# Tracing three score units of an attention beside the products of its values, in a two-layer diffusion trunk on one core

## The chip, the cores and the metric

The kernel runs on one core of a Trainium2 chip. The metric is the device time of one execution in microseconds (us). TensorE (PE in the rows) multiplies matrices, VectorE is DVE, ScalarE ACT, GpSimd POOL, and SyncE (SP) issues most transfers. Each engine works through an instruction queue of its own, fixed when the program is built, and instructions wait on semaphores that other engines raise.

## The reference

Two layers over 512 latent tokens and 256 context tokens, each with 1024 features. A layer normalises and modulates its input, projects it into four head groups, mixes each in its own way, projects the four results back and adds them; a convolutional channel mixer (ffn) follows.

```python
def attend(q, k, v, scale, sink=None):
    s = jnp.einsum('bqkgd,bnkd->bkgqn', q, k).astype(jnp.float32) * scale
    if sink is None:
        p = jax.nn.softmax(s, axis=-1)
    else:
        p = softmax_sink(s, sink)
    return jnp.einsum('bkgqn,bnkd->bqkgd', p.astype(v.dtype), v)
...
    ql = apply_axial_rope(rmsnorm(ql, q_norm), cos, sin)     # mixer A
    kl = apply_axial_rope(rmsnorm(kl, k_norm), cos, sin)
    kc = rmsnorm(kc, k_norm)
    k_all = jnp.concatenate([kl, kc], axis=1)
    v_all = jnp.concatenate([vl, vc], axis=1)
    y = dense_latent_attention(ql, k_all, v_all, scale)
```

Group A is a dense attention of four query heads over two key/value heads of 64 features. Group C is a banded one (keys within 128 positions, and the context) with a sink logit, B a state-space scan, D a latent attention. In layer 0 the context tokens are queries too.

## The kernel before

Everything stays in fp32 accuracy: an operand is split into a rounded high part and the rest (`hhi`/`hlo`, `whi`/`wlo`), and three products make one. `split` and `psplit` cast the high part on ACT and subtract on DVE (`split`) or POOL (`psplit`).

Per layer, `mixers` first makes the queries `aq0`, `aq1` and keys `ak` of A (the products `psf`, then sums `psn` and broadcasts `psr` for their norms, and DVE multiplications into `aq`, `ak`). Then come the values of A and C, six groups of 128 tokens with 24 products `psv` each; ACT copies each group into `vta` and `vtc`, DVE eight columns into `dtr`. Then `gqa` runs attention A in units of 128 queries, numbered u0, u1, ... in this text (in layer 0, 20 units: per head four latent ones of 768 keys and one of 2 x 128 context queries). A unit's scores are 4 products `pss`; DVE finds the negated maximum `nm`, ACT takes the exponential `p` and its sum, DVE inverts the sum, POOL multiplies (the function `scores`). LOOK = 3 units later `turn` transposes `p` through PE (`pspt`) and splits it, and `values` multiplies it with V (`psy`). Before its first scores a head pair needs `kh`/`kl` (the split keys) and `qh` (ACT casts the high half, POOL writes the low half by a subtraction); `get_kv` and `get_q` make them, and `prep` calls them for up to AHEAD = 10 units ahead.

Scores are in two PSUM tiles (`b2`), so u2 can begin when the exponential of u0 has read its tile. `psv`, `pspt`, `psy`, `psi` and `psn` share four smaller tiles (`b1`).

`run` takes streams with weights and interleaves what they trace: a stream of weight 0.3 advances 0.3 steps for each of one of weight 1. The build then simulates the traced program and fixes each engine's queue; an instruction behind a waiting one on the same engine waits too. Beside attention A runs `c_items`, the projections for C (`psi`); beside attention C run those of D and B.

Of the kernel before, what the change touches and what calls it, by code (L numbers as in the profile page):

```python
# [1 line left out]

# [1 line left out]

# [29 lines left out]
LOOK = 3  # L34
AHEAD = 10
NA, NC, NS = 0, 0, 12
WY = 4
WA, WC, WM, WD = 0.3, 0.3, 1.0, 1.0
# [4 lines left out]
STEP = 256  # L43
NP1 = 8
WP = 0.3
WQ, DQ = 0, 0
V0, V1, HC = 3, 0, 12
TK = 2
POOLK = (1, 3, 5, 7)
# [39 lines left out]
def trunk(ctx: ExitStack, tc: tile.TileContext, a, out):  # L89
# [22 lines left out]
    def s3(name, dt=F32, shape=(TOK,)):  # L112
        n = int(np.prod(shape))
        t = PW.tile([128, TOK], dt, tag="s3", name=name, bufs=N_S3)[:, :n]
        if len(shape) == 2:
            t = t.rearrange("p (a b) -> p a b", b=shape[1])
        elif len(shape) == 3:
            t = t.rearrange("p (a b c) -> p a b c", b=shape[1], c=shape[2])
        return t
# [20 lines left out]
    def psplit(hi, lo, src):  # L140
        act.copy(hi, src)
        pool.tensor_tensor(lo, src, hi.bitcast(F32), op=ALU.subtract)

    def run(*streams):

        live = [[g, w, 0.0] for g, w in streams]
        while live:
            s = min(live, key=lambda e: e[2])
            try:
                next(s[0])  # L150
                s[2] += 1.0 / s[1]
            except StopIteration:
                live.remove(s)
# [30 lines left out]
    def par_at(l, n, i=0, w=1):  # L184
        o, _ = POFF[n]
        return par[l][:, o + i:o + i + w]
# [253 lines left out]
    def gemm(items):  # L440

        posts = []

        def step():
            for g in list(posts):
                if next(g, posts) is posts:
                    posts.remove(g)

        w = items[0][0]()
        for i, (_, begin, *late) in enumerate(items):
            late = late[0] if late else 0
            quanta, post = begin(w)
            for q, _ in enumerate(quanta):
                if q == late and i + 1 < len(items):
                    w = items[i + 1][0]()
                step()
                yield
            if next(post, posts) is not posts:  # L460
                posts.append(post)
        while posts:
            step()
            yield
# [17 lines left out]
    def mixers(l, norm, halfway, mods):  # L482
# [124 lines left out]
        def once(f):  # L607
            box = []

            def g():  # L610
                if not box:
                    box.append(f())
                return box[0]

            return g

        def gqa(q, k, vt, sinkp, banded, ys):

            kmap = [(0, 256, 0), (512, 256, 256), (256, 256, 512)] if banded else [(0, TOK, 0)]
            cpos = 256 if banded else 512  # L620
            pos = (0, 1, 4, 5)
            halves = []
            for kv in range(2):
                r0 = slice(64 * kv, 64 * kv + 64)

                def get_kv(r0=r0, kv=kv):
                    kh, kl = s3("kh", F32R), s3("kl", F32R)
                    for s0, n, d0 in kmap:
                        for r in (slice(0, 64), slice(64, 128)):
                            act.copy(kh[r, d0:d0 + n], k[r0, s0:s0 + n])  # L630
                        for r in (slice(0, 64), slice(64, 128)):
                            pool.tensor_tensor(kl[r, d0:d0 + n], k[r0, s0:s0 + n], kh[r0, d0:d0 + n].bitcast(F32),
                                              op=ALU.subtract)
                    vhl = s3("vhl", F32R, (6, 128))
                    psplit(vhl[:, :, 0:64], vhl[:, :, 64:128], vt[:, :, 64 * kv:64 * kv + 64])
                    ys.append(s3("yf"))
                    return kh, kl, vhl, ys[-1]

                get_kv = once(get_kv)
                for hh in range(2):  # L640
                    hd = 2 * kv + hh
                    rh = slice(64 * hh, 64 * hh + 64)
                    rl = slice(64 - 64 * hh, 128 - 64 * hh)

                    def get_q(kv=kv, rh=rh, rl=rl):
                        qh = s3("qh", F32R)
                        act.copy(qh[rh, :QW], q[kv][rh, :QW])
                        pool.tensor_tensor(qh[rl, :QW], q[kv][rh, :QW], qh[rh, :QW].bitcast(F32), op=ALU.subtract)
                        return qh

                    get_q = once(get_q)

                    def prep(get_kv=get_kv, get_q=get_q):
                        get_kv()
                        get_q()

                    def sink(hd=hd):
                        return None if sinkp is None else (sinkp[0][:, hd:hd + 1], sinkp[1][:, hd:hd + 1])

                    def sc_mm(ps, q0, c0, w, masks=(), get_kv=get_kv, get_q=get_q):  # L660
                        kh, kl = get_kv()[:2]
                        qh = get_q()
                        qs = slice(q0, q0 + 128)
                        for o in range(0, w, 512):
                            n = min(512, w - o)
                            mm(ps[:, o:o + n], qh[:, qs], kh[:, c0 + o:c0 + o + n], True, False)
                            ms = [m for m in masks if o <= m[1] < o + n]
                            mm(ps[:, o:o + n], qh[:, qs], kl[:, c0 + o:c0 + o + n], False, not ms)
                            for i, (mi, mo) in enumerate(ms):
                                mm(ps[:, mo:mo + 128], cb[:, 0, :], cb[:, mi, :], False, i == len(ms) - 1)  # L670

                    def vhl(get_kv=get_kv):
                        return get_kv()[2]

                    def yf(get_kv=get_kv):
                        return get_kv()[3]

                    for hb in range(2):
                        def score(ps, qi, hb=hb, sc_mm=sc_mm):
                            i = 2 * hb + qi  # L680
                            if not banded:
                                sc_mm(ps, 128 * i, 0, TOK)
                                return TOK, 0
                            t0, t1 = ((0, 4), (0, 5), (1, 6), (2, 6))[i]
                            masks = []
                            if i > 0:
                                masks.append((1, (pos[i - 1] - t0) * 128))
                            if i < 3:
                                masks.append((2, (pos[i + 1] - t0) * 128))
                            sc_mm(ps, 128 * i, 128 * t0, 128 * (t1 - t0), masks)  # L690
                            return 128 * (t1 - t0), t0

                        if banded:
                            todo = [(2, 4, 0, 256)]
                            for j in range(4):
                                qb = [b for b in range(2) if abs(2 * hb + b - j) <= 1]
                                if qb:
                                    todo.append((pos[j], j, 128 * qb[0], 128 * qb[-1] + 128))
                            todo.append((3, 5, 0, 256))
                        else:  # L700
                            todo = ALL6
                        halves.append(Half(prep, score, todo, vhl, yf, hh, 256 * hb, sink, False))
                    if wc:
                        def score(ps, qi, sc_mm=sc_mm):
                            sc_mm(ps, 512 + 128 * qi, cpos, CTX)

                        halves.append(Half(prep, score, CTX2, vhl, yf, hh, SEQ, sink, True))
            return attention(halves)
# [30 lines left out]
        aq, ak = [s3("aq0"), s3("aq1")], s3("ak")  # L739
        cq, ck = [], []  # L740
        vta, vtc = [], []
# [4 lines left out]
        a_items = [first_item(norm, a_tiles, halfway)]  # L746
# [33 lines left out]
        v_items = [v_item(j) for j in range(6)]  # L780
# [435 lines left out]
        nsink = tiny("nsink", 4)  # L1216
        dve.tensor_scalar(nsink, par_at(l, "sink", 0, 4), -1.0, None, op0=ALU.mult)
        y_a, y_c = [], []
        run((gemm(a_items + v_items), 1.0))

        def some_mods(n):
            for _ in range(min(n, len(mods))):
                i, hc = mods.pop(0)
                yield from mod_chunks(i, [hc])

        run((gqa(aq, ak, vta[0], None, False, y_a), 1.0), (gemm(c_items), 0.3), (some_mods(NA), WA))
        run((gqa(cq, ck[0], vtc[0], (par_at(l, "sink", 0, 4), nsink), True, y_c), 1.0),
            (gemm(d_items + b_items), 1.5), (some_mods(NC), WC))
        yhi, ylo = [], []

# [357 lines left out]
```

## Time and profile before

| | |
|---|---|
| time, three runs | 1909.59, 1912.16, 1913.76 us; median 1912.16 |
| time of the profiled execution | 1908.92 us |
| its span, first to last instruction | 1907.1 us |
| mean granted TensorE clock | 0.977 |
| TensorE busy | 1802.8 us, 95% of the span |
| VectorE, ScalarE, GpSimd busy | 1112.1, 783.3, 543.7 us |

The profiled execution is 3.24 us quicker than the median. Its span leaves 1.8 us outside. TensorE's busy time is modelled at its matmuls' ends, so it is an upper reading.

### The profile page before, as it was taken

The numbers are of one execution on the slowest core, as the hardware profiler recorded it, in microseconds if no ns is written. First come the engines' busy times: TensorE is split into PE (matmuls) and PEld (weight loads), VectorE is DVE, ScalarE is ACT, GpSimd is POOL, SyncE is SP. The second block draws the span as 40 slices with busy tenths as digits, with TensorE's granted clock in tenths as the row PEclk, the third lists the DMA queues.
The fourth block names the chain that finished last, engine by engine and source line by source line (L and its number), as shares of the span: only waits on it lengthen the run. The fifth ranks groups of instructions, "written<-read, shape, count | busy, mean of one in ns | idle before, by whom it ended". The sixth has DMA issues, their size and how long they took to land.

```text
span 1907.1 us, 29376 instructions
## 1 busy us (share of the span) xinstructions
PE 1802.8 (95%) x11552; PEld 1568.0 (82%) x11552; DVE 1112.1 (58%) x2194; ACT 783.3 (41%) x1454; POOL 543.7 (29%) x579
## 2 busy tenths in 40 slices
PE   6989999878999999999999999999988999999997
PEld 3978898657888888888888888989767888888886
DVE  4664673967455545455454465667577565555545
ACT  3475563457343222222222255655357353323232
POOL 0363420655146133223230045441454210000001
PEclk9999999979999999999999999999979999999999
DMA  8101117203212222122221210103803322323221
GB/s 304 53 12 45 30 50 259 107 1 116 77 63 89 89 78 89 67 89 74 70 89 56 73 72 12 56 23 103 308 1 111 100 78 88 111 85 114 78 89 56
DMA packets 50569, 165.20 MB, mean 87 GB/s; under 512 B 5632, under 2 KB 9600, under 8 KB 50304
## 3 DMA queue, kind: packets, MB, share of 16 engines
q1 hardware_dynamic: 50432, 163.33, 24.9%
q8 instruction: 91, 1.49, 0.3%
q14 instruction: 46, 0.38, 0.1%
HBM read 159.12 MB, written 4.19 MB: 86 GB/s over the span
## 4 chain that ended last, share of the span: by engine, by line
PE 83%; DVE 9%; ACT 4%; issue 2%; DMA 1%; POOL 1%; SPq 0%; POOLq 0%; DVEq 0%; ACTq 0%
PE psi L134 41%; PE psd L134 16%; PE pso L134 5%; PE psf L134 3%; PE pss L134 3%; PE psy L134 3%; PE psm L134 2%; PE pspt L560 2%; PE psv L134 2%; ACT p L531 1%; DVE nm L524 1%; PE psq L134 1%; PE psn L134 1%; DVE ht L357 1%; DMA x<-in_xT_dram 1%
## 5 line engine op out<-in xcount | busy, mean ns | idle before, releaser
L134 PE MATMUL psi<-hhi,whi 128*128 128x256 f32 (+2 forms) x1600 | 491.9, 330 | 4.7 <-DVE fc L1344 2.5
L134 PE MATMUL psi<-hlo,whi 128*128 128x256 f32 (+2 forms) x1600 | 488.3, 328 | 0.0
L134 PE MATMUL psi<-hhi,wlo 128*128 128x256 f32 (+2 forms) x1600 | 487.8, 328 | 0.0
L138 DVE TENSOR_TENSOR wlo<-raw,whi 128x1024 fp32r<-128x1024 f32 (+2 forms) x188 | 238.8, 1270 | 151.4 <-ACT whi L137 108.9
L134 PEld LDWEIGHTS psi<-hhi,whi 128*128 128x128 f32 (+1 forms) x1600 | 288.5, 190 | 32.6 <-DVE fc L1344 2.7
L137 ACT CAST whi<-raw 128x1024 fp32r<-128x1024 f32 (+2 forms) x188 | 195.0, 1039 | 279.5 <-DMA raw<-in_wup_dram 109.2
L134 PEld LDWEIGHTS psi<-hhi,wlo 128*128 128x128 f32 (+1 forms) x1600 | 288.3, 190 | 26.2
L134 PEld LDWEIGHTS psi<-hlo,whi 128*128 128x128 f32 (+1 forms) x1600 | 288.4, 190 | 25.6
L1306 DVE SCALAR_TENSOR_TENSOR x<-psd,mod,x 128x512 f32<-128x512 f32 (+1 forms) x248 | 153.2, 644 | 179.1 <-PE psd L134 178.1
L323 POOL TENSOR_TENSOR sq<-sq,sq 128x256 f32<-128x256 f32 (+1 forms) x45 | 44.9, 999 | 554.0 <-ACT sq L321 532.8
L134 PE MATMUL psd<-ulo,whi 128*128 128x512 f32 (+1 forms) x552 | 167.8, 349 | 0.0
L134 PE MATMUL psd<-uhi,wlo 128*128 128x512 f32 (+1 forms) x552 | 167.4, 348 | 0.0
L134 PE MATMUL psd<-uhi,whi 128*128 128x512 f32 (+1 forms) x552 | 166.2, 348 | 0.0
L538 POOL TENSOR_SCALAR p<-p,sm 128x768 f32<-128x768 f32 (+3 forms) x120 | 100.0, 839 | 175.4 <-DVE sm L536 101.9
L531 ACT ACTIVATE p<-pss,nm 128x768 f32<-128x768 f32 (+3 forms) x120 | 93.0, 777 | 58.4 <-DVE nm L524 22.4
L227 POOL TENSOR_SCALAR mtmp<-wm,cact 128x256 f32<-128x256 f32 x112 | 62.5, 574 | 188.4 <-DMA wm<-in_wmod_dram 126.6
L1325 ACT ACTIVATE fc<-psi,par 128x512 f32<-128x512 f32 (+1 forms) x60 | 42.4, 707 | 176.4 <-PE psi L134 176.2
L524 DVE TENSOR_REDUCE nm<-pss 128x1 f32<-128x768 f32 (+2 forms) x96 | 84.7, 885 | 47.6 <-PE pss L134 47.4
L134 PEld LDWEIGHTS psd<-uhi,whi 128*128 128x128 f32 x552 | 94.4, 189 | 13.4
L134 PEld LDWEIGHTS psd<-uhi,wlo 128*128 128x128 f32 x552 | 93.7, 189 | 14.1
L134 PEld LDWEIGHTS psd<-ulo,whi 128*128 128x128 f32 x552 | 93.3, 188 | 13.5
L560 PE MATMUL pspt<-con,p 128*128 128x128 f32 x528 | 82.4, 277 | 4.3 <-POOL p L538 2.0
(271 smaller groups left out, 3330.3 us busy)
## 6 DMA issues: line engine op xcount, KB each, us to landing
wm<-in_wmod_dram SPq DMA_DIRECT2D x96, 512.0 KB, 6.8
raw<-in_wup_dram SPq DMA_DIRECT2D x88, 512.0 KB, 3.3
raw<-in_wdn_dram SPq DMA_DIRECT2D x44, 512.0 KB, 3.3
raw<-in_win_dram SPq DMA_DIRECT2D x34, 512.0 KB, 3.5
raw<-in_wout_dram SPq DMA_DIRECT2D x16, 512.0 KB, 3.3
x<-in_xT_dram SPq DMA_DIRECT2D x8, 384.0 KB, 8.1
x<-in_xT_dram SPq DMA_DIRECT2D x8, 256.0 KB, 7.6
xd<-x SPq DMA_DIRECT2D x8, 256.0 KB, 2.0
```

What stands on the lines that cost most here:

```text
L134: pe.matmul(out, lhsT, rhs, start=start, stop=stop, **kw)
L137: act.copy(hi, src)
L138: dve.tensor_tensor(lo, src, hi.bitcast(F32), op=ALU.subtract)
L227: pool.tensor_scalar(tmp[:, t], wm[:, g], cact[:, 4 * q + g, t:t + 1], 1.0, op0=ALU.mult, op1=ALU.mult)
L323: eng.tensor_tensor(self.sq[0][:, sl], self.sq[0][:, sl], sq[:, sl], op=ALU.add)
L357: dve.scalar_tensor_tensor(t, x[k][:, sl], self.sct[:, s, k:k + 1], self.ps[:, sl], op0=ALU.mult, op1=ALU.mult)
L524: dve.tensor_reduce(nm, ps[:, :width], axis=AX.X, op=ALU.max, negate=True)
L531: act.activation(p[:, i], v[:, i], AF.Exp, bias=nm[:, i:i + 1], accum_out=sm[:, i:i + 1])
L538: pool.tensor_scalar(p[:, i], p[:, i], sm[:, i:i + 1], 1.0, op0=ALU.mult, op1=ALU.mult)
L560: pe.transpose(pt[:, 128 * (j - j0):128 * (j - j0) + 128], p[:, 0, 128 * (j - t0):128 * (j - t0) + 128], ident)
L1306: dve.scalar_tensor_tensor(x[m][:, sl], p, mod[l][:, s, 40 + m:41 + m], x[m][:, sl], op0=ALU.mult, op1=ALU.add)
L1325: act.activation(c[:, b:e], p, AF.Identity, bias=par_at(l, "fcb", j), scale=par_at(l, "fcw", 3 * j + 1))
```

## The change

`get_kv` no longer splits V. A new `get_v`, run once per key/value head, does it, and `values` is the first to call it. So that the attention can be set up before V exists, `gqa` now takes the lists `vta` and `vtc` and looks into them only in `get_v`. The first `run` now covers only the queries and keys; a second one traces the value groups and, beside them at weight 0.2, the first three steps (LOOK) of attention A; a third continues it beside `c_items`. Attention C gets the later split of V alone. Two unused constants go. No product, exponential or transfer is added or taken away, and SyncE's queue is the same in both programs.

```diff
+from itertools import islice
...
-                    vhl = s3("vhl", F32R, (6, 128))
-                    psplit(vhl[:, :, 0:64], vhl[:, :, 64:128], vt[:, :, 64 * kv:64 * kv + 64])
-                    ys.append(s3("yf"))
-                    return kh, kl, vhl, ys[-1]
-
-                get_kv = once(get_kv)
+                    ys.append(s3("yf"))
+                    return kh, kl, ys[-1]
+
+                def get_v(kv=kv):
+                    vhl = s3("vhl", F32R, (6, 128))
+                    psplit(vhl[:, :, 0:64], vhl[:, :, 64:128], vt[0][:, :, 64 * kv:64 * kv + 64])
+                    return vhl
+
+                get_kv, get_v = once(get_kv), once(get_v)
...
-        run((gemm(a_items + v_items), 1.0))
+        run((gemm(a_items), 1.0))
...
-        run((gqa(aq, ak, vta[0], None, False, y_a), 1.0), (gemm(c_items), 0.3), (some_mods(NA), WA))
-        run((gqa(cq, ck[0], vtc[0], (par_at(l, "sink", 0, 4), nsink), True, y_c), 1.0),
+        att = gqa(aq, ak, vta, None, False, y_a)
+
+        run((gemm(v_items), 1.0), (islice(att, LOOK), 0.2))
+        run((att, 1.0), (gemm(c_items), 0.3), (some_mods(NA), WA))
+        run((gqa(cq, ck[0], vtc, (par_at(l, "sink", 0, 4), nsink), True, y_c), 1.0),
```

On TensorE, where attention A begins in layer 0: before, all 144 `psv` and then 48 products of the first `c_items` tile (`psi`) are done when the first scores come; these are the last three rows of those and the first two of the scores.

```order
L134 MATMUL psi<-hhi_277,whi 128x256 x2
L134 MATMUL psi<-hlo_285,whi 128x256 x2
L134 MATMUL psi<-hhi_277,wlo 128x256 x2
L134 MATMUL pss<-kh,qh 128x512
L134 MATMUL pss<-kl,qh 128x512
```

After, the scores of u0, u1 and u2 stand between the 96th and the 97th `psv`, and 48 `psv` come behind them (two rows of each).

```order
L134 MATMUL psv<-whi,hlo_285 128x264
L134 MATMUL psv<-wlo,hhi_277 128x264
L134 MATMUL pss<-kh,qh 128x512
L134 MATMUL pss<-kl,qh 128x512
L134 MATMUL pss<-kh,qh 128x256
L134 MATMUL pss<-kl,qh 128x256
...
L134 MATMUL psv<-whi,hhi_270 128x264
L134 MATMUL psv<-whi,hlo_278 128x264
```

So all 48 `psi` and a third of the `psv` are behind the first three units instead of ahead of them. The broadcasts `psr` stand 26 rows of PE's queue earlier in layer 0 and about where they were in layer 1; there the first three units are moved in the same way, and 48 `psv` come behind them too. Behind these 48, in layer 0, come u3 and u4, six `pspt`, u5 and u6, four `psi`, six `pspt`, u7 and then 27 `psi`; in layer 1 u3, six `pspt`, u4, u5 and u6, four `psi`, six `pspt`, u7 and then 22 `psi`.

On GpSimd, at the same place (`kl` and `qh` of the first heads, the low halves of V, the first multiplied `p`), before:

```order
L632 TENSOR_TENSOR kl<-ak,kh 64x768 x2
L142 TENSOR_TENSOR vhl<-vta,vhl 128x6x64
L648 TENSOR_TENSOR qh<-aq_258,qh 64x768 x2
L632 TENSOR_TENSOR kl<-ak,kh 64x768 x2
L142 TENSOR_TENSOR vhl<-vta,vhl 128x6x64
L648 TENSOR_TENSOR qh<-aq_259,qh 64x768
L538 TENSOR_SCALAR p<-p,sm 128x768 x4
```

and after:

```order
L632 TENSOR_TENSOR kl<-ak,kh 64x768 x2
L651 TENSOR_TENSOR qh<-aq_258,qh 64x768 x2
L632 TENSOR_TENSOR kl<-ak,kh 64x768 x2
L651 TENSOR_TENSOR qh<-aq_259,qh 64x768
L538 TENSOR_SCALAR p<-p,sm 128x768 x4
L651 TENSOR_TENSOR qh<-aq_259,qh 64x768
L538 TENSOR_SCALAR p<-p,sm 128x256 x2
L142 TENSOR_TENSOR vhl<-vta,vhl 128x6x64
```

The first `vhl` moves from ahead of the first `qh` to behind the first multiplied units. In attention C of layer 0, on the same engine (`cqk` holds the queries and keys of C), the queue after is

```order
L632 TENSOR_TENSOR kl<-cqk,kh 64x256 x6
L651 TENSOR_TENSOR qh<-cqk,qh 64x768 x2
L632 TENSOR_TENSOR kl<-cqk,kh 64x256 x6
L651 TENSOR_TENSOR qh<-cqk,qh 64x768
L538 TENSOR_SCALAR p<-p,sm 128x512
L538 TENSOR_SCALAR p<-p,sm 128x640 x2
```

where one `vhl` stood ahead of each first `qh` before. On TensorE there, 18 `psi` rows stand between u1 and u2 where ten stood, and u5, the first unit of the second head, comes behind 24 more `psi` rows.

On ScalarE the casts `kh`, `qh` now come first, then the load of the table for the exponential, the exponential of u0, the copies of four value groups, those of u1 and u2 and the last two groups' copies; the cast of the first `c_items` weights follows the exponentials of u3 and u4, while before it was done ahead of the value products.

## Rows read from the trace of the kernel before

**Rows 1.** The page: busy time by engine, and the chain that ended last.

```profile
PE 1802.8 (95%) x11552; PEld 1568.0 (82%) x11552; DVE 1112.1 (58%) x2194; ACT 783.3 (41%) x1454; POOL 543.7 (29%) x579
PE 83%; DVE 9%; ACT 4%; issue 2%; DMA 1%; POOL 1%; SPq 0%; POOLq 0%; DVEq 0%; ACTq 0%
```

**Rows 2.** Windows, layer 0: length, busy time by engine (instructions), granted clock, DMA share, GB/s.

```profile
102.00:106.00 4.00, 1.34 (x8) 0.98 (x6) 1.82 (x2) 2.27 (x4) 3.86 (x4) 1.00 0.00 0
106.00:110.00 4.00, 3.09 (x9) 2.41 (x10) 2.22 (x5) 1.93 (x5) 3.82 (x4) 0.53 0.00 0
110.00:114.00 4.00, 3.85 (x17) 3.31 (x17) 1.79 (x4) 3.68 (x9) 2.51 (x4) 0.62 0.00 0
...
130.00:160.00 30.00, 27.63 (x203) 24.15 (x202) 23.75 (x50) 20.91 (x51) 10.46 (x13) 1.00 0.12 37
```

**Rows 3.** Timeline of ScalarE, layer 0: start, us, instruction, idle time before and its releaser.

```profile
103.71 1.28 ACT L531 ACT_TABLE_LOAD   x1 [2.08 <-DVE nm L524]
105.01 0.90 ACT L531 ACTIVATE p<-pss,nm 128x768 f32<-128x768 f32 x1
```

**Rows 4.** TensorE, layer 0: its waits from 60 to 260 us (total, times, longest); timeline.

```profile
PE pss L134 <- ACT p L531: 7.9, 9, 2.7
...
106.05 0.66 PE L134 MATMUL pss<-kh,qh 128*128 128x512 f32 x1 [2.71 <-ACT p L531]
...
109.70 0.58 PE L134 MATMUL pss<-kh,qh 128*128 128x256 f32 x1 [0.85 <-ACT p L531]
```

**Rows 5.** Timelines of ScalarE and GpSimd, layer 0, before attention A.

```profile
88.03 1.69 ACT L630 CAST kh<-ak 64x768 fp32r<-64x768 f32 x2
90.42 0.27 ACT L771 COPY vta<-psv 128x128 f32<-128x128 f32 x1 [0.70 <-PE psv L134]
93.33 0.27 ACT L771 COPY vta<-psv 128x128 f32<-128x128 f32 x1 [2.47 <-PE psv L134]
...
88.94 3.76 POOL L632 TENSOR_TENSOR kl<-ak,kh 64x768 fp32r<-64x768 f32 x2 [18.48 <-ACT kh L630]
98.31 3.77 POOL L648 TENSOR_TENSOR qh<-aq,qh 64x768 fp32r<-64x768 f32 x2
```

**Rows 6.** Timeline of TensorE, layer 1, the first units of attention A.

```profile
1174.83 0.28 PE L134 MATMUL pss<-kl,qh 128*128 128x256 f32 x1
...
1177.19 0.50 PE L134 MATMUL pss<-kh,qh 128*128 128x512 f32 x1 [1.38 <-ACT p L531]
...
1180.33 0.47 PE L134 MATMUL pss<-kh,qh 128*128 128x512 f32 x1 [1.26 <-ACT p L531]
```

**Rows 7.** Timelines of ScalarE and GpSimd, layer 1, before attention A.

```profile
1162.89 0.27 ACT L771 COPY vta<-psv 128x128 f32<-128x128 f32 x1 [0.71 <-PE psv L134]
...
1161.40 3.75 POOL L632 TENSOR_TENSOR kl<-ak,kh 64x768 fp32r<-64x768 f32 x2 [10.86 <-ACT kh L630]
1170.77 2.66 POOL L648 TENSOR_TENSOR qh<-aq,qh 64x512 fp32r<-64x512 f32 x2
```

**Rows 8.** Windows, layer 1, columns as in rows 2.

```profile
1174.00:1178.00 4.00, 2.62 (x16) 2.09 (x14) 1.99 (x3) 2.63 (x5) 3.86 (x3) 1.00 0.00 0
1178.00:1182.00 4.00, 2.74 (x18) 2.24 (x16) 2.73 (x5) 3.33 (x8) 3.64 (x5) 1.00 0.01 2
...
1186.00:1230.00 44.00, 42.52 (x332) 39.76 (x331) 33.49 (x70) 28.79 (x63) 15.19 (x16) 1.00 0.13 43
```

**Rows 9.** Attention C of layer 0: TensorE's timeline, then a window.

```profile
195.27 0.39 PE L134 MATMUL pss<-kh,qh 128*128 128x256 f32 x1 [0.75 <-ACT p L531]
...
197.77 0.47 PE L134 MATMUL pss<-kh,qh 128*128 128x512 f32 x1 [1.76 <-ACT p L531]
...
198.00:202.00 4.00, 4.00 (x21) 3.72 (x21) 2.52 (x10) 3.65 (x11) 2.71 (x5) 0.57 0.01 2
```

**Rows 10.** TensorE's waits from 1120 to 1360 us: total, times, longest; GpSimd's timeline there.

```profile
PE pspt L560 <- POOL p L538: 2.0, 2, 1.7
...
1244.84 1.01 POOL L142 TENSOR_TENSOR vhl<-vtc,vhl 128x384 fp32r<-128x384 f32 x1
```

More of the change, by code (lines that the diff above doesn't have):

```diff
@@ L45 @@
 WP = 0.3
-WQ, DQ = 0, 0
 V0, V1, HC = 3, 0, 12
@@ L670, in sc_mm, with yf @@
                                 mm(ps[:, mo:mo + 128], cb[:, 0, :], cb[:, mi, :], False, i == len(ms) - 1)
-                    def vhl(get_kv=get_kv):
+                    vhl = get_v
+                    def yf(get_kv=get_kv):
                         return get_kv()[2]
-                    def yf(get_kv=get_kv):
-                        return get_kv()[3]
                     for hb in range(2):
```

## The prediction

> **What bounds the kernel now.** I read the page first: TensorE is busy 95% of the span and holds 83% of the chain that ended last [rows 1]. A change that neither adds nor takes away a product can move the time only through TensorE's idle stretches and through its granted clock. So I looked for both around the places that the change touches: the windows of the two starts of attention A, then the timelines of the engines there, then the same for attention C.
>
> Layer 0, attention A: TensorE does u0 and u1 and then stands 2.71 us until the exponential of u0 has read its tile [rows 4]. The reader sees why it is so long in ScalarE's timeline: the load of the exponential's table waits for the first maximum and lies on the path, 1.28 us from 103.71 to 104.99, before the first exponential at 105.01 [rows 3]. TensorE has nine waits of this kind between 60 and 260 us, 7.9 us; four of them, 4.0 us, are here (0.85 is the next in the rows, two small ones follow) [rows 4]. And the clock falls: the 8 us behind the gap have 0.53 and 0.62, the windows before and after it 1.00 [rows 2]. 0.5 is the lower level, 1.2 of 2.4 GHz. What it costs: 16 `pss` and six `pspt` ran in that stretch, the first 512-wide `pss` behind the gap at 0.66 us against 0.50 in layer 1, where the clock held [rows 4, 6]. Counting stretch by stretch, I put it at 2.6 us (an estimate: four 0.7 us units' worth of work at half speed, 2.8, less what lay beside the wait for the exponential).
>
> Layer 1, attention A: gaps of 1.38 and 1.26 us, 0.3 more behind them (2.0 less 1.7 in rows 10) [rows 6, 10], and the clock stays at 1.00 through both windows [rows 8]. The table load was ahead of time here. So a gap of 1.4 us cost only itself, one of 2.7 us also the clock.
>
> Attention C: in layer 0 three gaps, 0.75 and 1.76 in the rows and 0.6 before them, 3.1 us, and the clock at 0.57 for 4 us behind the last [rows 9]; in layer 1 one of 1.70 us, `pspt` waiting for the `p` that GpSimd had not multiplied, because a `vhl` of 1.01 us was ahead of it [rows 10].
>
> **The change part by part.** *Where TensorE arrives, layer 0.* The fourth value group's copy came at 90.42 [rows 5], 96 products done, and the new order has the same work ahead of that place, so TensorE comes to u0 at about 90.0. u0 needs `kh`, `kl` and the first `qh`. The keys `ak` are ready about 3 us earlier than before, since the `psr` stand 26 rows earlier, at 2.91 us for 24 rows (the distance of two copies, rows 5: 93.33 less 90.42) 3.1 us. So `kh` begins at 85.0 instead of 88.03, `kl` is done at 85.8 + 3.76 = 89.6, and the first `qh`, half of 3.77, at 91.5 [rows 5]. Before, 5.6 us passed between the end of `kl` (92.7) and `qh` (98.31), which stood behind the split of V; now nothing lies between. TensorE waits 91.5 less 90.0 = 1.5 us, which is new.
>
> *The first units.* u0 and u1 take 0.7 us each. u2 waits for u0's exponential. In layer 1, with the table loaded early, u2 began 2.36 us after u0's last `pss` began (1177.19 less 1174.83), a gap of 1.38 [rows 6]. The new order has the table load ahead of the first exponential and behind nothing that depends on the scores, so I take 1.4 us for both layers. Then 48 `psv`, 5.8 us, run without a wait, and beside them the softmax of the three units ends on DVE, ACT and GpSimd. Behind them u3, u4 and six `pspt` cover about 1.1 us of the next 2.36, so u5 waits about 1.3, u6 0.55 and the first `psi` 1.1, because the cast of its weights is now queued on ScalarE behind two exponentials (0.90 each, rows 3) and was done long ahead before. That is 1.5 + 1.4 + 1.3 + 0.55 + 1.1 = 5.9 against 4.0: **+1.9** (0, if the later ones are covered, to 3). The 48 `psi` that covered GpSimd before are not lost; they come later as cover.
>
> *The clock in layer 0.* Before, 2.6 us went there. After, no single gap is as long as 2.7, but 1.5 and 1.4 come 1.4 us apart and a second cluster of three gaps follows. The nearest rows are attention C (0.6, 0.75, 1.76 in 5 us: it fell, rows 9) and layer 1 (1.38 and 1.26, 1.8 us apart: it held, rows 8). Ends: 0 and two falls, 5. I take 2.9, so **+0.3** (−2.6 to +2.4).
>
> *Attention A, layer 1.* TensorE is at u0 when the fourth copy starts, 1162.9. Here the `psr` did not move, `kl` ends at 1161.40 + 3.75 = 1165.15, and half of `qh`, 1.33, follows: 1166.5 [rows 7]. TensorE waits 3.6 us with 48 ready `psv` queued behind it. Then u2 1.4, and a later cluster of 0.8, 0.95 and 0.35: 7.1 against 3.0, **+4.1** (2 to 4.5). The gap of 3.6 is longer than any in rows 4 to 9, and the one of 2.7 brought the clock down; I add **+2**, half of the 4 us of products that come before it returns (ends 0 and 3.5, as a 7 us stretch at 0.5 in rows 2).
>
> On this gap the Trainium skill speaks against the change: "TensorE: Matmul & The Clock Gate", section "HAM oscillation — how this bites in real kernels", says that a loop whose bursts of products are parted by waits drops back to the low clock at each wait and pays for the climb every time. The two gaps of layer 1, with the clock at 1.00, are short cases where that did not happen; by the page alone the new long one costs a fall, as in my sum.
>
> *Attention C, layer 0.* `vhl` is off GpSimd (1.01 in rows 10) and ScalarE before the first `p`, 18 instead of ten `psi` lie between u1 and u2, and u5 has 24 more `psi` ahead of it, 2.8 us at 0.12: its gap of 1.76 goes, the others stay, **−1.7**. With that gap gone I expect the clock to hold: 4 us at 0.57 cost 1.7, of which I take **−1.2** (0 to −1.7). *Layer 1:* the 1.70 is shorter than `vhl` and the wait for `qh` that fall away, **−1.7** (−2 to 0).
>
> *Given back.* 17 (layer 0) and 44 (layer 1) more products of `c_items` are left to fill gaps later. Between 130 and 160 TensorE lost 2.4 us [rows 2], between 1186 and 1230 1.5 [rows 8]. I take **−1** in each, ends 0 and −1.9. The splits of V cost nothing later: GpSimd is busy 10.5 of 30 us there [rows 2], against the 1.0 of a `vhl`; without that cover each would cost 1.0.
>
> Sum: 1.9 + 0.3 + 4.1 + 2 − 1.7 − 1.2 − 1.7 − 2 = +1.7. If every term fell to one end it would be −10 or +13; the terms are not so tied, except through the clock, and the rivals below take it up. Against the profiled execution's 1908.92 that is 1910.6; it was 3.24 quicker than the median of the three runs, so I carry the difference to the median: 1912.16 + 1.7 = 1913.9. Small swaps in the order of the scan and latent-attention stages have no sign that I can read; I take them as ±2.
>
> **The rivals.** *Slower.* The clock falls after each new pair of gaps, in both layers, and the later filling gives nothing. Layer 0: 5 instead of 2.9 (+2.1); layer 1: 3.5 instead of 2 (+1.5); no giving back (+2); attention C keeps its fall (+1.2): +8.5, 1920.7. For it: three gaps in 5 us brought it down [rows 9]. Against: two gaps of 1.3 did not [rows 8].
>
> *Faster.* The early softmax of three units under 48 `psv` removes the whole second cluster (2.95 in layer 0, 2.1 in layer 1), since `p` of u0 to u2 are ready for `pspt` and ScalarE has nothing else to do, and with it the clock holds in layer 0 (−2.9): 1.7 − 5.05 − 2.9 = −6.2, 1905.9. It is decided by the order in which ScalarE takes the exponentials of u3 and u4 against the weights' cast; if the cast and u3's exponential end within the 1.1 us that `pspt` and u4 last, it happens. Against: 2.36 is longer than that.
>
> *One wait for another.* Gaps shift and the totals stay, as TensorE's products are the same: ±0, 1912.2.
>
> **How the numbers follow.** My forecast has a chance of 0.4, the slower rival 0.25, the faster one 0.2, and the even exchange 0.15. A measurement of this kernel tells about 0.2% from no change, 3.8 us: 1908.3 to 1916.0. The forecast, ±3 around 1913.9, lies within with 0.3 of its 0.4 and above with 0.08, below with 0.02; the even exchange lies within. So faster 0.22, same 0.45, slower 0.33. The range 1906 to 1921.5 leaves out half of each outer rival. I predict 1914.
>
> **What would show it.** In the profile after: TensorE idle before u0 in both layers, 1.5 and 3.6 us, released by GpSimd's `qh`; 1.4 before u2; the clock below 1 behind the 3.6 and not behind layer 0's attention C; the 1.70 before `pspt` gone. It would be wrong if the wait before u0 is under 1 us in layer 1 (GpSimd's `kl` earlier than I place it), if the clock drops nowhere, or if the time goes or comes in the later stages, where the order shows only swaps.

## The result, and the profile after

The changed kernel takes 1932.44 us (median of four runs, 1930.45 to 1935.12) against 1912.39 for the kernel before: a ratio of 1.0106, 95% interval 1.0088 to 1.0123. It is 20 us slower; predicted were 1914, with a range of 1906 to 1921.5. The profiled execution took 1931.23 us, with a span of 1929.4.

The page of the changed kernel, busy times and chain, against [rows 1]:

```profile
PE 1814.1 (94%) x11552; PEld 1576.0 (82%) x11552; DVE 1117.9 (58%) x2194; ACT 782.2 (41%) x1454; POOL 541.7 (28%) x579
PE 81%; DVE 8%; ACT 4%; issue 3%; DMA 2%; POOL 1%; SPq 0%; POOLq 0%; DVEq 0%; ACTq 0%
```

TensorE ran the same 11552 instructions in 1814.1 us instead of 1802.8, at a mean granted clock of 0.965 instead of 0.977. So by the profile, which models the ends of products, the span grew by 22.3 us, of which 11.3 are the same products taking longer and 11.0 are idle time.

Where? Windows cut at the same work in both traces: attention stage of layer 0, its scan and latent attention, attention stage of layer 1, its scan and latent attention. Length, then busy time by engine (TensorE, its weight loads, VectorE, ScalarE, GpSimd), granted clock, DMA share, GB/s. Before:

```profile
33.87:319.31 285.44, 273.00 (x2119) 251.90 (x2120) 175.10 (x428) 156.76 (x349) 99.84 (x96) 0.98 0.19 67
319.31:477.65 158.34, 130.40 (x1033) 101.86 (x1031) 118.03 (x288) 90.10 (x211) 82.02 (x85) 0.92 0.28 101
...
1121.50:1348.00 226.50, 218.88 (x1685) 204.17 (x1686) 150.12 (x366) 128.77 (x278) 85.56 (x80) 0.98 0.19 63
1348.00:1474.95 126.95, 111.94 (x892) 87.30 (x891) 92.68 (x239) 73.97 (x172) 63.86 (x69) 0.91 0.32 118
```

After:

```profile
34.86:327.05 292.19, 277.17 (x2118) 256.93 (x2119) 176.68 (x428) 155.81 (x349) 99.53 (x96) 0.95 0.19 65
327.05:482.14 155.09, 131.23 (x1033) 102.11 (x1031) 116.58 (x288) 90.51 (x211) 82.63 (x85) 0.92 0.28 103
...
1127.43:1366.50 239.07, 222.16 (x1684) 207.02 (x1685) 154.44 (x368) 128.93 (x279) 83.76 (x80) 0.96 0.19 62
1366.50:1497.18 130.68, 114.94 (x893) 87.52 (x891) 93.39 (x239) 74.16 (x172) 63.71 (x69) 0.90 0.31 114
```

Layer 0's attention stage is 6.8 us longer, layer 1's 12.6; the scans are 3.3 shorter and 3.7 longer. The rest of the 22.3 (2.5) is in the start and between the two layers.

TensorE's timeline at the start of attention A, layer 0 and then layer 1, against [rows 4, 6]:

```profile
96.41 0.50 PE L134 MATMUL pss<-kh,qh 128*128 128x512 f32 x1 [1.35 <-POOL qh L651]
...
99.45 0.50 PE L134 MATMUL pss<-kh,qh 128*128 128x512 f32 x1 [1.38 <-ACT p L531]
...
109.42 0.50 PE L134 MATMUL pss<-kh,qh 128*128 128x512 f32 x1 [1.35 <-ACT p L531]
...
112.52 0.79 PE L134 MATMUL psi<-hhi,whi 128*128 128x256 f32 x2 [0.75 <-ACT whi L137]
...
1170.93 0.50 PE L134 MATMUL pss<-kh,qh 128*128 128x512 f32 x1 [3.42 <-POOL qh L651]
...
1173.97 0.50 PE L134 MATMUL pss<-kh,qh 128*128 128x512 f32 x1 [1.38 <-ACT p L531]
...
1183.51 0.50 PE L134 MATMUL pss<-kh,qh 128*128 128x512 f32 x1 [0.73 <-ACT p L531]
```

The waits before u0 and u2 are there, of the length forecast. Three windows tell of the clock: a stretch without any wait ahead of them (0.50), the one behind the second pair of waits in layer 0 (0.51), and the 10 us behind the wait of 3.42 in layer 1 (1.00):

```profile
74.00:80.00 6.00, 6.00 (x28) 6.00 (x29) 3.12 (x32) 0.00 (x0) 0.00 (x0) 0.50 0.02 7
...
111.00:118.00 7.00, 6.25 (x27) 5.72 (x26) 5.71 (x8) 4.55 (x8) 5.46 (x5) 0.51 0.00 1
1170.93:1180.93 10.00, 8.62 (x62) 8.11 (x63) 3.71 (x11) 6.11 (x19) 9.56 (x8) 1.00 0.00 0
```

In attention C, layer 0 and then layer 1, against [rows 9, 10], TensorE, then ScalarE and GpSimd in layer 0:

```profile
209.34 0.38 PE L134 MATMUL psy<-phi,vhl 128*128 128x256 f32 x1 [2.73 <-POOL vhl L142]
...
1273.26 1.09 PE L280 MATMUL psr<-con,ny 128*128 128x128 f32 x4 [2.51 <-DVE sm L535]
...
1320.96 0.50 PE L134 MATMUL pss<-kh,qh 128*128 128x512 f32 x1 [1.78 <-ACT p L531]
1322.62 0.38 PE L134 MATMUL psy<-phi,vhl 128*128 128x256 f32 x1 [0.85 <-POOL vhl L142]
...
206.79 0.69 ACT L531 ACTIVATE p<-pss,nm 128x512 f32<-128x512 f32 x1 [1.20 <-DVE mqn L846]
...
207.66 0.50 ACT L141 CAST vhl<-vtc 128x384 fp32r<-128x384 f32 x1
...
208.30 0.99 POOL L142 TENSOR_TENSOR vhl<-vtc,vhl 128x384 fp32r<-128x384 f32 x1 [2.64 <-ACT vhl L141]
```

This is what the forecast did not have. The first value product of C stands 2.73 us for V's low half. GpSimd had been idle 2.64 us, waiting for the high half; ScalarE casts that only behind the exponential of u5, which waits for u5's scores and their maximum (the row names `mqn`, which VectorE did right behind it). V itself had been in `vtc` since 106.7, for 101 us.

In layer 1 the late split shows in another way. Before, the first ten `psy` of C stood ahead of the four `psr`; now the build's order has the `psr` ahead of the `psy`, and TensorE stands 2.51 us at the `psr`, until VectorE has done the steps of their norm, between which steps of the softmax stand in its queue.

At the end of attention A in layer 1 (timeline of TensorE) a row of gaps follows one another:

```profile
1222.14 1.00 PE L560 MATMUL pspt<-con,p 128*128 128x128 f32 x6 [0.83 <-DVE plo L138]
...
1224.06 0.38 PE L134 MATMUL psy<-phi,vhl 128*128 128x256 f32 x1 [0.92 <-ACT phi L137]
...
1226.00 0.33 PE L134 MATMUL psy<-plo,vhl 128*64 128x256 f32 x1 [1.12 <-DVE plo L138]
```

### The profile page after: what moved, and what is told of

It reads as the page before. It is cut to its first block, busy times and chain, and to the rows that moved or that the text cites. A ratio compares the mean times of both kernels' runs of the same rounds, so it can differ in the third digit from the quotient of the medians.

```text
span 1929.4 us, 29345 instructions
## 1 busy us (share of the span) xinstructions
PE 1814.1 (94%) x11552; PEld 1576.0 (82%) x11552; DVE 1117.9 (58%) x2194; ACT 782.2 (41%) x1454; POOL 541.7 (28%) x579
## 4 chain that ended last, share of the span: by engine, by line
PE 81%; DVE 8%; ACT 4%; issue 3%; DMA 2%; POOL 1%; SPq 0%; POOLq 0%; DVEq 0%; ACTq 0%
PE psi L134 41%; PE psd L134 16%; PE pso L134 5%; PE psy L134 3%; PE pss L134 3%; PE psf L134 3%; PE psm L134 2%; PE pspt L560 2%; ACT p L531 1%; DVE nm L524 1%; PE psq L134 1%; PE psv L134 1%; DMA x<-in_xT_dram 1%; DVE wlo L138 1%; DVE ht L357 1%
```

## The experiments

Every ratio is to the kernel before, on the same chip; us are worked out from it at 1911. The edits start from the changed kernel.

**The first four: which part of the change is slow.** `c_early` splits V of attention C in `get_kv` again; attention A's order on TensorE is the changed kernel's.

```diff
-                get_kv, get_v = once(get_kv), once(get_v)
+                get_v = once(get_v)
+
+                def get_kv(kv2=get_kv, v=get_v):
+                    got = kv2()
+                    if banded:
+                        v()
+                    return got
+
+                get_kv = once(get_kv)
```

> The changed kernel with V split early again in attention C only (in get_kv, as before); attention A stays as changed, its queues the same as in the changed kernel. Theory 1 (the late split of V in C is a cost of its own: the cast of vhl stands behind exponentials on ScalarE and the first psy waits for it, 2.73 and 0.85 us, with the clock falling behind them): no wait of psy for vhl in C, the clock dips at 1270 and 1323 smaller, about 8 to 10 us quicker than the changed kernel, some 1923. Theory 2 (the time comes from the early scores of A alone, and C only inherits a delay): within 3 us of the changed kernel, 1929 to 1933, the waits in C replaced by the 1.7 us ones of before.

Measured: 1920.6, ratio 1.0049 (1.0033 to 1.0065), +9. So 11 of the 20 us come back with C's split: theory 1.

`late_only` keeps both late splits and takes the early scores away.

```diff
-        run((gemm(a_items), 1.0))
+        run((gemm(a_items + v_items), 1.0))
...
-        run((gemm(v_items), 1.0), (islice(att, LOOK), 0.2))
```

> V split late in A and C, but no scores beside the value products: the queries, keys and all value groups are traced first, as before, then attention A from its start beside c_items. Theory 1: the C part of the loss stays, 8 to 10 us, and A's part (the waits before u0, u2, u5 and the clock at 73 to 80 us) goes: about 1920. Theory 2: no loss without the early scores: 1909 to 1913.

Measured: 1930.46, ratio 1.0101 (1.0073 to 1.0128), +19. A miss for both theories as I had put them: without any early scores the kernel is about as slow. In the trace `psy` waits for `vhl` in attention A too, 2.62 us in layer 0 and 1.07 in layer 1. The late split costs in each attention; in the changed kernel the first value product of A comes later (120.2 us against 113.7) and does not wait for it.

`two_units` traces two steps beside the value products.

```diff
-        run((gemm(v_items), 1.0), (islice(att, LOOK), 0.2))
+        run((gemm(v_items), 1.0), (islice(att, 2), 0.2))
```

> The changed kernel with two steps of the attention beside the value products instead of three. u0 to u2 still stand together ahead of the last 48 psv, but the psn of layer 0 are spread between psv again as before, and 24 psi stand between those psv and u3. Theory 1 (27 psn rows of two columns in a row brought the clock down from 73.7 to 80.5 us): clock 1.00 there, 3.5 us back; the waits before u0 and u2 remain at 1.4 and 1.4 (layer 0), 3.4 and 1.4 (layer 1); no wait before u5 and the first psi; about 1925. Rival (the fall has to do with something else at that place, such as the start of the value products): the clock falls there as in the changed kernel, and at most 2 us come back.

Measured: 1945.49, ratio 1.0187 (1.0153 to 1.0221), +36. On the clock the expectation held: the windows from 70 to 94 us, with the `psn` spread, are at full clock,

```profile
70.00:80.00 10.00, 10.00 (x86) 10.00 (x86) 7.43 (x39) 2.02 (x6) 1.73 (x2) 1.00 0.01 2
80.00:94.00 14.00, 11.66 (x131) 10.83 (x129) 3.36 (x8) 4.72 (x6) 3.83 (x3) 1.00 0.00 1
94.00:105.00 11.00, 8.58 (x34) 7.71 (x34) 3.56 (x10) 6.68 (x17) 10.69 (x8) 0.53 0.00 0
```

but TensorE, earlier at u0, now waited 3.96 us there, and the clock fell behind that instead. On the time it was a miss of 20 us: `vhl` is waited for in A (1.26 and 1.19) and C (2.96, 0.56 and 0.85), and `psr` in layer 1's C waits 3.97 behind DVE's softmax. Against the changed kernel its profile is 8.5 us longer in layer 0's scan (163.6) and 5.5 in layer 1's attention (244.6), and 4.0 shorter in layer 1's scan (126.7). Why the scan grew was not tested.

`two_groups_first` traces two value groups with the queries and keys.

```diff
-        run((gemm(a_items), 1.0))
+        run((gemm(a_items + v_items[:2]), 1.0))
...
-        run((gemm(v_items), 1.0), (islice(att, LOOK), 0.2))
+        run((gemm(v_items[2:]), 1.0), (islice(att, LOOK), 0.2))
```

> The changed kernel with the first two value groups traced with the queries and keys; four groups then run beside the three steps. The psn of layer 0 still stand in a row. u0 and u1 now stand 34 psv (layer 0) or 36 and more (layer 1) later, and 14 or 11 psv lie between u1 and u2. If the wait before u0 is one for GpSimd's chain of kl and qh with a fixed end, as read in the trace: it is 0 in both layers, that before u2 under 0.5, so 1.35 + 3.4 + 1.5 to 2 are saved: about 1925, with the clock still falling at 73 us. Rival (what is saved there is lost at the next units, as fewer products are left behind them): waits of 1 us and more before u3 and u4, and 1929 to 1933.

Measured: 1926.13, ratio 1.009 (1.0055 to 1.0126), +17; the median is the 1925 expected, and one of the four runs, at 1936.9, makes the interval wide. There is no wait before u0 in either layer; 1.28, 0.68 and 1.31 remain before later units in layer 0, 0.76 in layer 1.

**The next four: each part alone on the kernel before.** The edits are the two above, with conditions on the attention or the layer: `c_late` has the first (`a_late`, in its place, `if banded`), `l1_only` the second (`l0_only`, in its place, 0).

```diff
+                    if not banded:
+                        v()
...
+        if l == 1:
+            run((gemm(v_items), 1.0), (islice(att, LOOK), 0.2))
```

> The kernel before, with V split late in attention C alone; attention A and its start are as before. Theory 1 (the late split in C is a cost of its own, which two of the runs so far put at 10 to 12 us by difference): 1921 to 1923, with psy waiting for vhl in both layers and a clock fall behind each. Rival (C loses only when attention A before it was shifted, so that its start falls differently beside the projections for D and B): 1910 to 1914.

Measured: 1922.69, ratio 1.0059 (1.0039 to 1.008), +11. Theory 1. Its timeline of TensorE, and the windows of its two attention stages:

```profile
206.19 0.58 PE L134 MATMUL psy<-phi,vhl 128*128 128x256 f32 x1 [3.83 <-POOL vhl L142]
...
1264.68 1.09 PE L280 MATMUL psr<-con,ny 128*128 128x128 f32 x4 [3.97 <-DVE sm L535]
...
34.51:324.07 289.56, 273.95 (x2119) 252.76 (x2120) 175.71 (x428) 156.30 (x349) 98.90 (x96) 0.96 0.19 66
1126.46:1357.37 230.91, 218.28 (x1687) 203.92 (x1687) 152.54 (x368) 129.58 (x279) 84.67 (x80) 0.98 0.19 62
```

> The kernel before, with V split late in attention A alone, and no scores beside the value products; C is as before. The order that the build makes of it spreads the first scores between the first 48 psi (nine psi, u0, 15 psi, u1, ...). Theory 1 (costs add): 1930 less the 11 of C, 1919. Rival (the spread start has no gap of 1.3 us and more, so A gains, and C's late split has a larger price when it comes behind it): 1908 to 1912.

Measured: 1916.23, ratio 1.0024 (1.0011 to 1.0037), +5, between the two. The 2.71 of [rows 4] is gone: u0 to u5 begin without a wait. But u6 and u7 wait 1.47 and 0.91 for exponentials, and `psy`, which here stands behind u7, waits for `vhl`, 2.62 in layer 0 (the row) and 1.22 in layer 1.

```profile
113.81 0.58 PE L134 MATMUL psy<-phi,vhl 128*128 128x256 f32 x1 [2.62 <-POOL vhl L142]
```

> The early scores (three steps beside the value products, V of A split late) in layer 0 only; layer 1 and attention C of both layers as before. From the stages of the run with C early: layer 0's attention stage 2.3 us longer, its scan 3.0 shorter, so 1909 to 1913, no difference that can be told, although the clock falls behind the psn in a row. Rival (each layer carries half of the 9.6): 1915 to 1917.

Measured: 1910.42, ratio 1.001 (0.9994 to 1.0026): no difference, as expected.

> The early scores in layer 1 only, V of A split late there; layer 0 and attention C of both layers as before. From the stages of the run with C early: the wait of 3.4 before u0, 0.8 to 1.4 before u2, 0.7 and 0.7 after it, and six gaps of 0.3 to 1.0 at the end of attention A with a clock fall behind them: 9 to 12 longer, 1920 to 1923. Rival: 1915 to 1917, as half of the 9.6.

Measured: 1923.59, ratio 1.0066 (1.0044 to 1.0089), +13. So the change's parts alone are +11 (C), +13 (early scores in layer 1) and +2 (layer 0, interval −1 to +5): 26, with some 4 of uncertainty on each, for the change's 20: they add up within the noise. In the profile of `l1_only` the clock did fall behind u0's wait, and again at the end of A:

```profile
1165.32 0.79 PE L134 MATMUL pss<-kh,qh 128*128 128x512 f32 x1 [3.40 <-POOL qh L659]
...
1164.00:1175.00 11.00, 8.88 (x35) 8.01 (x36) 3.56 (x10) 6.93 (x18) 10.51 (x10) 0.53 0.00 0
1222.00:1230.00 8.00, 6.88 (x38) 6.64 (x37) 5.28 (x10) 2.78 (x7) 2.73 (x3) 0.57 0.20 66
```

**Curing each cause.** `c_ask_sooner` is `c_late`, `ask_sooner` is `late_only`, each with the split asked for behind the second unit's scores.

```diff
                     got[i] = scores(*units[i])
+                    if 0 < i:
+                        units[i - 1][0].vhl()
```

> The kernel before with V split late in attention C alone, as in the run of that, but asked for right behind the scores of a head's second unit instead of at the first value product: the cast of vhl then stands on ScalarE behind the exponential of u1 instead of that of u5. Theory 1 (the 11 us of the late split in C are what psy waits for vhl, 3.83 and 0.56 in layer 0 and 0.85 in layer 1, with what these waits push and the clock behind them): those waits are gone, 1908 to 1913, at or under the kernel before, as GpSimd's chain ahead of the first p is 1 us shorter. Rival (C loses through the other order of its projections and its norm's products, with psr waiting 3.97 behind DVE's softmax in layer 1): 1917 to 1922.

Measured: 1907.36, ratio 0.998 (0.9966 to 0.9994), −4. One call moved by four units makes 15 us between `c_late` and this. ScalarE casts V at 191.10, with 1.30 us of idle time right behind it, and the same value product waits for its `phi`, not for V:

```profile
191.10 0.52 ACT L141 CAST vhl<-vtc 128x384 fp32r<-128x384 f32 x1
...
200.13 0.39 PE L134 MATMUL psy<-phi,vhl 128*128 128x256 f32 x1 [0.54 <-ACT phi L137]
...
33.02:315.18 282.16, 269.78 (x2119) 249.20 (x2120) 174.64 (x427) 156.39 (x349) 100.02 (x96) 0.98 0.20 68
1116.44:1343.00 226.56, 220.25 (x1685) 205.73 (x1686) 150.83 (x367) 129.16 (x278) 86.15 (x80) 0.97 0.19 64
```

The windows are its attention stages: 7.4 and 4.4 us shorter than those of `c_late`. In layer 1 the call moved more than the cast: the build's order has the `psy` ahead of the `psr` again, and the 3.97 is gone with the rest. So the rival that named this wait had a part of the loss right, but the wait hangs on the late call too. The two ways, cast and order, were not parted.

> V split late in attentions A and C, asked for right behind the scores of a head's second unit; no scores beside the value products. The first scores of A are then spread between psi, as in the run with A late, which lost 4 to 6 us, and psy's wait for vhl of 1.07 there should be gone. Theory 1 (the late split costs through psy's waits for vhl): 1908 to 1914. Rival (A loses because the 48 psi are used up before the first units): 1915 to 1920.

Measured: 1898.23, ratio 0.9925 (0.9903 to 0.9948): 14 us quicker than the kernel before and the best of all. Its stages (attention of layer 0 and of layer 1), and its waits from 90 to 125 us:

```profile
33.03:311.14 278.11, 268.28 (x2118) 248.44 (x2119) 173.88 (x427) 155.93 (x349) 100.28 (x96) 0.98 0.20 70
...
1113.06:1337.29 224.23, 219.51 (x1686) 205.50 (x1687) 152.05 (x366) 128.67 (x278) 87.81 (x80) 0.97 0.20 64
...
PE pss L134 <- ACT p L531: 0.7, 2, 0.4
```

With V's split behind the first `qh`, the build's order has `psi` between the first units (nine, u0, 15, u1, 17, u2), so each exponential passes under products. That much `a_late` had too. What the earlier call adds is that `psy` now begins behind u5 instead of u7 and parts u5 from u6: the longest of the waits for exponentials from 90 to 125 us is 0.4, none is for `vhl`, and the clock does not fall there. Layer 0's stage is 7.3 us shorter than before. That A is the larger part of the 14 follows from `c_ask_sooner`'s −4; A alone was not run.

`l1_kl_on_dve` and `l1_weight_02` start from `l1_only`.

```diff
-                            pool.tensor_tensor(kl[r, d0:d0 + n], ...
+                            eng = dve if l == 1 and not banded and r.start else pool
+                            eng.tensor_tensor(kl[r, d0:d0 + n], ...
...
-        run((att, 1.0), (gemm(c_items), 0.3), (some_mods(NA), WA))
+        run((att, 1.0), (gemm(c_items), 0.2 if l == 1 else 0.3), (some_mods(NA), WA))
```

> The early scores in layer 1 only, and there the second of the first two subtractions for kl (and of the next head pair's) on DVE instead of GpSimd, so that the first qh follows one kl instead of two; PE's order is the same up to a few psi. If the 3.4 us before u0 are GpSimd's chain, 1.6 to 1.8 remain. Theory 1 (the loss of 13 in layer 1 is in equal parts the start, 2.6 with a clock fall behind it, and the end of attention A, 3 with a fall): the start's fall goes too, 4 to 6 back, 1918 to 1920. Rival A (the start is the whole loss): 1911 to 1914. Rival B (the wait moves to the next unit): 1922 to 1925.

Measured: 1919.41, ratio 1.0041 (1.0026 to 1.0057), +8: 5 of 13 back, a difference that the two intervals just allow to be none. The wait before u0 is 2.40, not the 1.6 to 1.8 expected: GpSimd's one `kl`, beside which VectorE now does the other (0.95 us from 1164.66), takes 2.59, where in `l1_only` two took 3.70.

```profile
1164.71 2.59 POOL L633 TENSOR_TENSOR kl<-ak,kh 64x768 fp32r<-64x768 f32 x1 [12.54 <-ACT kh L630]
1160.35 3.70 POOL L632 TENSOR_TENSOR kl<-ak,kh 64x768 fp32r<-64x768 f32 x2 [10.96 <-ACT kh L630]
```

> The early scores in layer 1 only, with the projections for C traced at weight 0.2 instead of 0.3 beside the rest of attention A in layer 1. The start is the same instruction for instruction; 48 psi are left for the end of attention A, as in the kernel before, instead of 24 some units earlier. Theory 1 (the gaps of 0.5 to 1.1 at the end of A come of psi used up too soon, and the clock falls behind them): no such row of gaps, 4 to 7 back, 1917 to 1920. Rival (the end loses no time on balance, the gaps only move to the middle units, which now have no psi between them): 1922 to 1926.

Measured: 1918.48, ratio 1.0031 (1.0016 to 1.0046), +6: 7 of 13 back. The gaps of 0.83, 0.92 and 1.12 are gone; 0.48 and 0.46 are the longest left at the end of A. That end (16 us, more products) has 1.44 us idle, where the changed kernel's (the second row, 14 us) had 3.92:

```profile
1214.00:1230.00 16.00, 14.56 (x119) 13.61 (x119) 13.15 (x26) 9.44 (x19) 6.03 (x4) 1.00 0.27 96
...
1214.00:1228.00 14.00, 10.08 (x77) 8.51 (x76) 10.12 (x20) 7.58 (x18) 4.49 (x5) 1.00 0.25 76
```

`l1_both` has both edits.

> The early scores in layer 1 only, with both cures of the two runs before together there: the second copy of kl on DVE, and the projections for C at weight 0.2. Theory 1 (the 13 us of layer 1 are the start and the end of attention A, and no more): the two savings of 4 to 7 add, 1911 to 1915. Rival (both saved the same clock fall, so they don't add, or something in the early order itself costs): 1917 to 1920.

Measured: 1916.37, ratio 1.0028 (1.0017 to 1.0039), +5. Together the savings are 7, not 12; with 2 to 4 us of uncertainty on each of the four runs, that they don't add is not shown. The waits that are left in its trace are 2.40 before u0, 0.80 before u2 and 0.73, 0.69 and 0.89 behind them. So the start was cured only in part, and the 5 that stay (+3 to +7) can lie in these waits or elsewhere in the early order.

`change_ask_u3` is the whole change with the split asked for behind the fourth unit.

```diff
                     got[i] = scores(*units[i])
+                    if i >= LOOK:
+                        units[i - LOOK][0].vhl()
```

> The changed kernel, whole, with V split asked for right behind the scores of a head's fourth unit instead of at the first value product two units later; attention A's order is the same but for a few psi. Theory 1 (the 11 us of the late split in C come from the two exponentials ahead of the cast): psy's waits for vhl under 1 us each, 1920 to 1924. Rival (any later place than before the scores costs the 11): 1929 to 1934.

Measured: 1927.71, ratio 1.008 (1.0061 to 1.01), +15: 5 of the 11 back (give or take 5), less than expected, though no `psy` waits for `vhl` any more. Its two attention stages, 287.6 and 238.8 us, are as long as those of `c_early`, 287.7 and 239.0, which is 6 us quicker by the ratios; the profiles differ in the scans (157.2 and 132.3 against 155.3 and 127.4).

## Why the prediction was wrong

**The step that failed** is the sentence "The splits of V cost nothing later". I priced GpSimd's 1.0 us and looked for room on GpSimd. What counted was where the cast stands on ScalarE: asked for at the first value product, it is behind the exponential of u5, and TensorE waits for the pair (2.73 in the changed kernel); in layer 1 the value products, waiting for V, went behind the `psr`, and TensorE waits there (2.51). So attention C, put at −4.6 (−1.7, −1.2, −1.7), gives +11 in `c_late`. `c_ask_sooner` shows the cause: with the call moved, −4 (−6.5 to −1). That this is about the forecast term is partly luck: against the kernel before, its profile has all of it in layer 0 (282.2 against 285.4) and nothing in layer 1 (226.6 against 226.5), where −1.7 was forecast. Of the forecast itself, the 1.76 before C's u5 and the 1.70 before `pspt` did go. The −1.2 for the clock in layer 0's C did not come: it fell there as well, to 0.65 behind the wait for V:

```profile
209.00:213.00 4.00, 3.66 (x21) 3.66 (x22) 1.57 (x4) 1.69 (x4) 1.24 (x3) 0.65 0.00 0
```

**Arrival and first waits**: right in length. 1.35, 1.38, 1.35 and 0.75 in layer 0 (forecast 1.5, 1.4, 1.3, 1.1), 3.42, 1.38, 0.73 and 0.68 in layer 1 (3.6, 1.4, 0.8, 0.95). That the first wait kept its length is in part luck: TensorE came to u0 at 95.1 instead of 90.0 (1.0 of it from the start of the program, some 3.4 from the clock, below), and GpSimd's `kl` began as much later, at 90.8 instead of 85.8.

**The clock in layer 0**: its size was off. Beside the fall behind the gaps (111 to 118) there is one from 74 to 81 us with no gap at all, about 3.4 us of products lost. There 28 `psn`, which stood in groups of at most eight before, run in a row; the forecast has no term for them. `l0_only` has them too, and its layer 0 attention stage is 3.4 us longer in the profile (288.8 against 285.4); over its ten runs that is within the noise (−1 to +5).

**The clock in layer 1**: half a fall, +2, was the right kind of term for something that is not certain. Behind its 3.42 us the changed kernel's profile has 1.00 over the 10 us from u0 on. The same wait, of 3.40 to 3.42 us, gave 0.54 there in `l1_only`, 0.52 in `change_ask_u3`, and 0.84 to 0.85 in `c_early`, `l1_weight_02` and `two_units`. The Trainium skill, "TensorE: Matmul & The Clock Gate", section "HAM oscillation — how this bites in real kernels", has each such wait pay a fall; of these six profiles five agree.

```profile
1165.32:1175.32 10.00, 9.20 (x37) 8.33 (x38) 3.56 (x10) 5.65 (x16) 9.56 (x8) 0.54 0.00 0
1165.97:1175.97 10.00, 9.21 (x58) 8.44 (x59) 3.70 (x11) 5.96 (x18) 9.57 (x8) 0.84 0.00 0
```

**Given back**: wrong in sign for layer 1. I took the 44 `psi` that were left as cover; the order uses them up in the middle units, and the end of A has gaps of 0.83, 0.92 and 1.12. `l1_weight_02`, which leaves them for the end, gets 7 us back (6.7, give or take 5). In layer 0 the early scores alone measure as nothing, against a forecast of +2.2 less 1.

**The scans**: taken as ±2, they moved by −3.3 and +3.7. No experiment took them by themselves, but five profiles bound what they can tell. In `l1_only`, `l1_kl_on_dve`, `l1_weight_02` and `l1_both` every compute engine has the same queue in layer 0's scan as in the kernel before, and its length is 157.9, 161.0, 160.9 and 160.9 us against 158.3. The row is that of `l1_kl_on_dve`, with a clock of 0.89 where the kernel before had 0.92:

```profile
320.69:481.69 161.00, 134.12 (x1032) 104.56 (x1031) 118.00 (x288) 90.22 (x211) 82.17 (x85) 0.89 0.27 99
```

So 3 us in a scan come and go between profiles with the same order, and the −3.3 and +3.7 are not shown to be the change's.

Of the rivals the slower one came nearest in time, for another reason. What stays open: 5 us of layer 1's early order after both cures, and 6 us between `change_ask_u3` and `c_early`, which no wait of TensorE in attention C accounts for.

## What to carry to other kernels

Work that is put off until its first use goes behind whatever its engines have been given by then: ask for it a few steps before, in a stretch in which they are idle, and check the place in each engine's queue, not only the engine's load, and what the build now puts ahead of the work that waits for it. A long wait at the head of an in-order engine is cured by products between the dependent steps (`psi` between u0, u1 and u2), not by starting those steps sooner with nothing ready behind them. When cover is spent early, look at who needed it last.

## What the runs showed of the hardware

A TensorE that the profile shows as busy can lose its clock: 28 products of two columns in a row (from 71.45 us, 4.0 us long), with no idle time, were followed by a granted clock of 0.50 from 74 to 80 us. With the same products in groups of at most eight it stayed at 1.00. All five profiles with the row (`c_early`, `two_groups_first`, `l0_only`, `change_ask_u3` and the changed kernel) have the fall, 0.50 to 0.64 from 74 to 78 us; in the other eleven the clock holds there.

```profile
71.45 3.98 PE L134 MATMUL psn<-con,sq 128*128 128x2 f32 x28
```

How much is lost is not fixed by the order: in `c_early`, with the same order up to there and the row begun 2 us sooner, these 6 us had 0.76 and the 6 behind them 1.00.

```profile
74.00:80.00 6.00, 6.00 (x50) 5.85 (x51) 2.58 (x27) 0.00 (x0) 0.00 (x0) 0.76 0.00 0
```

A subtraction on GpSimd can take longer beside one on VectorE: 64x768 elements took 1.85 us each in `l1_only` (3.70 for two) and 2.59 in `l1_kl_on_dve`, where VectorE did an equal one in the same microsecond. One pair of rows shows it, above; why was not tested.
